# Fifteen tiles of the feed-forward's first product by seven block products (Strassen), with weight sums built in DRAM

## The chip, the cores and the metric

The kernel runs on one core of one Trainium2 chip. The metric is device time in microseconds (us). Every time below that is not a time of a whole run is read from one profiled execution of the kernel before.

## The reference, cut to what matters

One inference step of a decoder: 512 prompt tokens and 64 sample tokens (8 sequences of 8), 576 rows in all, 1024 features, float32. The part that the change rewrites is the last sub-layer:

```python
xn = rms_norm(x, g[4])
gate, up = jnp.split(xn @ w_ffn_in, 2, axis=-1)          # w_ffn_in: 1024 x (2 x 2816)
x = x + rms_norm((jax.nn.silu(gate) * up) @ w_ffn_out, g[5])   # w_ffn_out: 2816 x 1024
```

Ahead of it stand an in-projection of 1024 to 6144 columns, a gated convolution and a gated recurrence, their output projections and merge, and a cross-attention into 256 memory tokens, each with norms before and after.

## The kernel before

**Layout.** Activations stand with 128 features on the partitions and the 576 tokens along the free axis; the columns come as halves of 288 (`HN`), or, between the mix and the end, as half A (320 columns: the samples and half of the prompt) and half B (256 columns).

**Products.** TensorE works on pairs: `split` (L101) makes of a float32 tile a rounded high part on ScalarE (L102) and the rest on VectorE (L103), and `mm3` (L105) makes of each 128x128 block of weights three matmuls, high by high (L106), high by low (L107) and low by high (L108). A tile of 128 output features over 1024 input features is thus 8 x 3 matmuls for each half of the columns.

**Weight stream.** SyncE (SP) loads one 128x1024 tile of weights (512 KB, rows of 512 bytes) at L165 into `wraw` (5 buffers), and `w_prep` (L169) splits it into `whi` and `wlo` (4 buffers each). A step's products call for the split of the tile three steps ahead, and that for the load two further ahead:

```python
def w_prep(upto, dma_ahead=2):
    ...
    i = ptr["prep"]
    w_dma(i + dma_ahead)
    ...
    w_prep((w[0] if w else nextw) + 3)      # in run_steps, ahead of each step's products
```

The first tiles are split by ScalarE (L360) and GpSimd (L361).

**Stages.** Start (x loaded, normed and transposed); eight column tiles `c` of the in-projection (`in_u`, `in_hc`, `in_hh`, `in_gate`, `in_hb`: four weight tiles and the gate's blocks for each `c`); branches out and merge; mix; memory keys and values, queries, attention in an order written out by hand; feed-forward in; feed-forward out. In the in-projection GpSimd splits the gate's blocks (`gate_w`, L469 and L470), copies and clears small pieces (L485 to L492, L537, L538, L544, L585 to L593). GpSimd also issues the few transfers of activations to DRAM (L841, L943, L969, L1191, L1269), on a queue of its own, q0 in the profile; SyncE's loads are q1.

**Feed-forward in.** 22 column tiles `j`. Tiles 0 to 6 run half A ahead of half B's attention output (`ffn_half`); tiles 7 to 21 as two steps each, `ffn_gate` (L1226) and `ffn_up` (L1239), 2 x 48 matmuls of alternately 320 and 256 columns, PSUM tiles `mm` of two banks.

**Feed-forward out.** 8 output tiles `n`, each in three groups of k (8, 8 and 6 of the 22 tiles) that accumulate in PSUM, `ffo`; the last two tiles are done by halves, (6, A), (7, A), (6, B), (7, B), so that the end of half A (`rb_a`, `y_a`, `out_a`) stands among products of half B. `last` does tile 7 of half B with the sums of squares (L1379), the last scale (L1396) and the stores.

**Order.** The program is written in steps; a scheduler then orders each engine's own instructions by priority and by what it expects to be ready, so an instruction that waits for nothing can stand much earlier on its engine than it is written. Every engine runs its own list strictly in order.

Of the kernel before, what the change touches and what calls it, by code (L numbers as in the profile page):

```python
# [9 lines left out]
F32 = mybir.dt.float32  # L10
# [5 lines left out]
D = 1024  # L16
# [23 lines left out]
# Background work (ns) let in behind a step.  # L40
# [12 lines left out]
def decoder_step(  # L53
# [18 lines left out]
    # ---------------------------------------------------------------- storage  # L72
# [76 lines left out]
    # ---------------------------------------------------------------- weight stream  # L149
    wsrc = []  # L150

    def w_cols(w, r0, nk, c0, ncol, as_is=False):
        src = w[r0:r0 + nk * 128, c0:c0 + ncol].rearrange("(k p) c -> p k c", p=128)
        wsrc.append((src, nk, ncol, as_is))
        return len(wsrc) - 1
# [4 lines left out]
    def w_dma(upto):  # L160
        while ptr["dma"] <= min(upto, len(wsrc) - 1):
            i = ptr["dma"]
            src, nk, ncol, _ = wsrc[i]
            t = wraw_p.tile([128, 1024], F32, tag="wraw", name="wraw")
            nc.sync.dma_start(out=t[:, :nk * ncol].rearrange("p (k c) -> p k c", c=ncol), in_=src)  # L165
# [3 lines left out]
    def w_prep(upto, dma_ahead=2):  # L169
        while ptr["prep"] <= min(upto, len(wsrc) - 1):  # L170
# [5 lines left out]
            ptr["prep"] += 1  # L176
            if as_is:
                ready[i] = t
                continue
# [6 lines left out]
    # ---------------------------------------------------------------- program order  # L186
# [34 lines left out]
    # ---------------------------------------------------------------- constants  # L221
# [42 lines left out]
    def rows_rstd(o, j, m):  # L264
        """rs[:, j:j+m] from the sums of squares there; columns from o on are scratch."""
# [12 lines left out]
    def startup():  # L278
        log_exp()
        # x: token tiles, the first three of them ahead of everything else  # L280
# [49 lines left out]
        def sums(i):  # L330
            """rs[:, i]: sum of squares, one half of the columns on each engine."""
# [93 lines left out]
        # transposed vectors  # L425
# [47 lines left out]
    # ---------------------------------------------------------------- in-projection  # L473
# [145 lines left out]
    for c in range(KT):  # L619
# [10 lines left out]
        step(wi(0), *in_hb(c), budget=9000)  # L630

# [870 lines left out]
```

## Time and profile before

| what | us |
|---|---|
| three runs | 1180.17, 1181.19, 1181.98 (median 1181.19) |
| profiled execution, span from its first to its last instruction | 1179.4 |
| the median of the runs beyond that span | 1.8 |
| TensorE busy | 1159.2 (98%) |
| VectorE, ScalarE, GpSimd busy | 609.5, 555.2, 119.2 |

The profiled execution's time of its own is its span, 1179.4; the page gives no other, and the runs' times hold what lies around a span as well. All sums are made against 1179.4, and 1.8 is added to set a result beside the runs.

How to read the profile: TensorE is busy all the time but for a few us at the start and the end. The chain of work that ended last shows which engine the end waited for at each moment; idle time of the other engines costs nothing by itself.

### The profile page before, as it was taken

The numbers are of one execution on the slowest core, as the hardware profiler recorded it, in microseconds if no ns is written. First come the engines' busy times: TensorE is split into PE (matmuls) and PEld (weight loads), VectorE is DVE, ScalarE is ACT, GpSimd is POOL, SyncE is SP. The second block draws the span as 40 slices with busy tenths as digits, with TensorE's granted clock in tenths as the row PEclk, the third lists the DMA queues.
The fourth block names the chain that finished last, engine by engine and source line by source line (L and its number), as shares of the span: only waits on it lengthen the run. The fifth ranks groups of instructions, "written<-read, shape, count | busy, mean of one in ns | idle before, by whom it ended". The sixth has DMA issues, their size and how long they took to land.

```text
span 1179.4 us, 20915 instructions
## 1 busy us (share of the span) xinstructions
PE 1159.2 (98%) x8704; PEld 1139.8 (97%) x8704; DVE 609.5 (52%) x926; ACT 555.2 (47%) x924; POOL 119.2 (10%) x253
## 2 busy tenths in 40 slices
PE   6999999999999999999999999999999999999997
PEld 4999999999999999999998899999999999999997
DVE  6666555652223335787768768974323323212235
ACT  5665655652122226676567777764322222222233
POOL 5332222202000000113200000000000000000000
PEclk9999999999999999999999999999999999999999
DMA  8323222222323345566765775665333232232352
GB/s 234 92 86 90 73 77 86 72 85 85 90 73 89 93 149 164 175 190 203 226 212 197 228 224 149 207 179 158 109 100 89 83 90 67 81 86 81 92 159 90
DMA packets 234635, 150.76 MB, mean 128 GB/s; under 512 B 7817, under 2 KB 222873, under 8 KB 234539
## 3 DMA queue, kind: packets, MB, share of 16 engines
q1 hardware_dynamic: 231300, 141.03, 40.7%
q0 software_dynamic: 2432, 7.04, 1.6%
q10 hardware_dynamic: 806, 1.34, 0.4%
q8 instruction: 68, 1.11, 0.4%
q14 instruction: 29, 0.23, 0.1%
HBM read 139.99 MB, written 9.40 MB: 127 GB/s over the span
## 4 chain that ended last, share of the span: by engine, by line
PE 95%; DMA 2%; ACT 1%; DVE 1%; issue 0%; POOL 0%; SPq 0%; DVEq 0%
PE mm L106 29%; PE mm L107 29%; PE mm L108 29%; PE aux L1099 1%; PE aux L1083 1%; DMA wraw<-in_cache_mem_v_dram 1%; PE aux L106 1%; PE aux L107 1%; PE aux L108 1%; DMA wraw<-in_w_in_dram 1%; PE aux L831 0%; PE aux L385 0%; DMA wraw<-in_w_o_x_dram 0%; PE aux L768 0%; POOL wlo L361 0%
## 5 line engine op out<-in xcount | busy, mean ns | idle before, releaser
L106 PE MATMUL mm<-u,whi 128*128 128x288 f32 (+2 forms) x2506 | 745.7, 298 | 0.0
L108 PE MATMUL mm<-u,wlo 128*128 128x288 f32 (+2 forms) x2506 | 742.2, 296 | 1.1 <-POOL wlo L361 1.1
L107 PE MATMUL mm<-u,whi 128*128 128x288 f32 (+2 forms) x2506 | 741.8, 296 | 0.0
L108 PEld LDWEIGHTS mm<-u,wlo 128*128 128x128 f32 x2506 | 474.3, 189 | 1.7 <-POOL wlo L361 1.5
L107 PEld LDWEIGHTS mm<-u,whi 128*128 128x128 f32 x2506 | 474.5, 189 | 1.2 <-DVE u L389 0.3
L106 PEld LDWEIGHTS mm<-u,whi 128*128 128x128 f32 x2506 | 474.4, 189 | 1.0 <-ACT u L388 0.2
L102 ACT CAST whi<-wraw 128x1024 fp32r<-128x1024 f32 (+1 forms) x229 | 237.8, 1039 | 486.7 <-PE mm L107 301.0
L103 DVE TENSOR_TENSOR wlo<-wraw,whi 128x1024 fp32r<-128x1024 f32 (+1 forms) x229 | 277.6, 1213 | 323.9 <-ACT whi L102 320.4
L102 ACT CAST u<-u 128x320 fp32r<-128x320 f32 (+6 forms) x116 | 54.3, 500 | 68.2 <-DVE u L543 26.3
L103 DVE TENSOR_TENSOR u<-u,u 128x320 fp32r<-128x320 f32 (+6 forms) x116 | 60.2, 542 | 15.7 <-ACT u L102 15.5
L1252 DVE TENSOR_TENSOR u<-u,mm 128x320 f32<-128x320 f32 (+1 forms) x30 | 12.3, 451 | 64.1 <-PE mm L108 64.1
L103 DVE TENSOR_TENSOR u<-aux,u 128x512 fp32r<-128x512 f32 (+2 forms) x60 | 32.8, 585 | 3.8 <-ACT u L102 3.7
L102 ACT CAST u<-aux 128x512 fp32r<-128x512 f32 (+2 forms) x60 | 28.0, 515 | 5.7 <-DVE u L103 2.1
L106 PE MATMUL aux<-u,u 128*128 128x256 f32 (+1 forms) x96 | 27.8, 294 | 0.0
L108 PE MATMUL aux<-u,u 128*128 128x256 f32 (+1 forms) x96 | 27.6, 288 | 0.0
L107 PE MATMUL aux<-u,u 128*128 128x256 f32 (+1 forms) x96 | 27.6, 288 | 0.0
L841 POOL DMA_DIRECT2D x_s<-u x8 | 4.5, 561 | 227.1 <-DVE u L832 226.9
L673 DVE TENSOR_TENSOR u<-u,mm 128x576 f32<-128x576 f32 x8 | 6.0, 754 | 33.8 <-PE mm L108 33.8
L653 DVE TENSOR_TENSOR u<-u,mm 128x576 f32<-128x576 f32 x8 | 6.0, 755 | 30.1 <-PE mm L108 30.1
L496 DVE SCALAR_TENSOR_TENSOR u<-u,vecs,u 128x600 f32<-128x600 f32 x24 | 20.2, 842 | 2.5 <-ACT u L494 1.9
L590 DVE TENSOR_TENSOR u<-mm,u 128x64 f32<-128x64 f32 (+2 forms) x24 | 7.3, 352 | 27.1 <-PE mm L108 27.1
L720 DVE TENSOR_TENSOR u<-u,u 128x640 f32<-128x640 f32 (+1 forms) x24 | 18.6, 778 | 0.9 <-ACT u L719 0.9
(250 smaller groups left out, 951.4 us busy)
## 6 DMA issues: line engine op xcount, KB each, us to landing
wraw<-in_w_ffn_in_dram SPq DMA_DIRECT2D x58, 512.0 KB, 3.8
wraw<-in_w_in_dram SPq DMA_DIRECT2D x48, 512.0 KB, 3.8
wraw<-in_w_ffn_out_dram SPq DMA_DIRECT2D x20, 512.0 KB, 3.9
wraw<-in_w_mix_out_dram SPq DMA_DIRECT2D x16, 512.0 KB, 4.3
wraw<-in_w_kv_x_dram SPq DMA_DIRECT2D x16, 512.0 KB, 4.1
wraw<-in_w_q_x_dram SPq DMA_DIRECT2D x16, 512.0 KB, 4.3
wraw<-in_cache_mem_k_dram SPq DMA_DIRECT2D x16, 512.0 KB, 4.3
wraw<-in_cache_mem_v_dram SPq DMA_DIRECT2D x16, 512.0 KB, 4.4
```

The lines of the kernel that those rows point to most:

```text
L102: ACT.copy(hi, src)
L103: DVE.tensor_sub(lo, src, f(hi))
L106: PE.matmul(out, lhsT=wh, rhs=xh, start=start, stop=False)
L107: PE.matmul(out, lhsT=wh, rhs=xl, start=False, stop=False)
L108: PE.matmul(out, lhsT=wl, rhs=xh, start=False, stop=stop)
L496: DVE.scalar_tensor_tensor(uc[:, :NU], up[:, k:k + NU], wcb(k, c), uc[:, :NU], op0=ALU.mult, op1=ALU.add)
L590: DVE.tensor_mul(o, i, src if a else src.rearrange("p (b t) -> p b t", t=8))
L653: DVE.tensor_mul(both(t), both(t), box.pop("yr")[:, :, :HN])
L720: DVE.tensor_add(M[key][:, :n], M[key][:, :n], s[:, :n])
L1083: PE.transpose(ps[:, d * 256 + i * 128:d * 256 + (i + 1) * 128], kr[i][:, h * 256 + d * 128:h * 256 + (d + 1) * 128], ident)
L1099: PE.matmul(ps[0:m], lhsT=t[:, k * 64:k * 64 + m], rhs=src, **kw)
L1252: DVE.tensor_mul(t[:, hs(h)], t[:, hs(h)], ps[:, h, :w])
```

## The change

- **Feed-forward in, tiles 7 to 21.** Each tile's gate and up columns, the even and odd input tiles, and the left and right halves of the 576 columns make a 2x2 by 2x2 block product. It is done with seven block products in place of eight (`ffn_pair`): EG, s1, s2, OG, s3, s4, OU, each 4 k-tiles x 3 matmuls of 288 columns. EG, s2, s3 and OU accumulate one after the other in bank 0 of one PSUM tile (each is copied out or used before the next is added), s1 and s4 in bank 1, OG in an `aux` tile. Copies and sums behind them: p1, p5, p6 on ScalarE, p2, p7, p3, p4 on VectorE.
- **Sums of activations.** `x3_sums` builds four sums of the normed input in background work (VectorE and ScalarE), 4 times.
- **Sums of weights.** `s1` to `s4`, each 512 rows x 1920 columns in DRAM, are made from `w_ffn_in` by 32 DMAs of 128 rows (0.983 MB each) that GpSimd issues: 16 plain copies and 16 that add to what stands there (`accum_op`). They are written two behind each `c` of the in-projection and one behind each step pair of the branches.
- **Weight loads of that stage.** A 128x1024 tile now holds two blocks of 4 k-tiles and comes by two DMAs of 256 KB (`w_blocks`); 53 tiles in place of 30 for the fifteen `j`.
- **Feed-forward out.** k in groups of 7, 7 and 8; the first two groups follow right behind their `j` and are kept in SBUF (`fs`, copied by ScalarE, then added by VectorE); in the last group the weights of tiles 3 to 7 are kept, half A of tiles 3 to 7 is done first, then half B.

```diff
+    def w_blocks(srcs):
+        wsrc.append((srcs, 4 * len(srcs), 128, False))
...
             t = wraw_p.tile([128, 1024], F32, tag="wraw", name="wraw")
-            nc.sync.dma_start(out=t[:, :nk * ncol].rearrange("p (k c) -> p k c", c=ncol), in_=src)
+            n = nk * ncol // len(srcs)
+            for j, src in enumerate(srcs):
+                nc.sync.dma_start(out=t[:, j * n:(j + 1) * n].rearrange("p (k c) -> p k c", c=ncol), in_=src)
...
+            if as_is == "keep":
+                hi, lo = new(F32R, 2), new(F32R, 2)
+                for j in range(2):
+                    split(hi[j][:, 0:512], lo[j][:, 0:512], t[:, j * 512:(j + 1) * 512])
+                ready[i] = Halves(hi), Halves(lo)
+                continue
...
+    sums = {n: tc.dram_tile([512, DFF - NB * 128], F32, name=f"sum_{n}") for n in ("s1", "s2", "s3", "s4")}
+    def sum_task(op, n, src, i):
+        def go():
+            r = slice(i * 128, i * 128 + 128)
+            if src in sums:
+                a = sums[src][r, :]
+            else:
+                k = 2 * i + (src[0] == "O")
+                c = (src[1] == "U") * DFF
+                a = w_ffn_in[0][k * 128:(k + 1) * 128, c + NB * 128:c + DFF]
+            kw = {"accum_op": ALU.add} if op == "add" else {}
+            nc.gpsimd.dma_start(out=sums[n][r, :], in_=a, **kw)
+        return go
+    sum_tasks = deque(
+        sum_task(op, n, src, i)
+        for stage in ((("copy", "s1", "EU"), ("copy", "s3", "EG")), (("add", "s1", "OU"), ("add", "s3", "EU")),
+                      (("copy", "s2", "s3"),), (("add", "s2", "OU"),), (("copy", "s4", "s2"),), (("add", "s4", "OG"),))
+        for op, n, src in stage for i in range(4))
+    def sum_step():
+        if sum_tasks:
+            step([], sum_tasks.popleft(), budget=0)
...
         step(wi(0), *in_hb(c), budget=9000)
+        for _ in range(2):
+            sum_step()
...
         step([w_cols(w_rnn_out[0], 0, KT, n * 128, 128)], *br_rnn(n))
...
+        sum_step()
...
         step([w_cols(w_conv_out[0], 0, KT, n * 128, 128)], *br_conv(n))
+        sum_step()
...
+    def x3_sums(i):
+        def go():
+            a, b = x3f[2 * i], x3f[2 * i + 1]
+            DVE.tensor_sub(a[:, L], a[:, L], a[:, R])
+            DVE.tensor_sub(a[:, R], b[:, R], a[:, R])
+            DVE.scalar_tensor_tensor(b[:, R], a[:, L], -1.0, b[:, R], op0=ALU.mult, op1=ALU.subtract)
+            DVE.scalar_tensor_tensor(b[:, L], b[:, R], -1.0, b[:, L], op0=ALU.mult, op1=ALU.subtract)
+            for k, t in ((2 * i, a), (2 * i + 1, b)):
+                t_h[k], t_l[k] = new(F32R), new(F32R)
+                split(t_h[k][:, 0:T], t_l[k][:, 0:T], t[:, 0:T])
+            free(a, b)
+        return go
...
+    def product(W, b, ps, X, xs, first, last):
+        wh, wl = W
+        xh, xl, o = X
+        for i in range(4):
+            k, x = 4 * b + i, 2 * i + o
+            PE.matmul(ps, lhsT=wh[:, k, :], rhs=xh[x][:, xs], start=first and i == 0, stop=False, skip_group_check=True)
+            PE.matmul(ps, lhsT=wh[:, k, :], rhs=xl[x][:, xs], start=False, stop=False, skip_group_check=True)
+            PE.matmul(ps, lhsT=wl[:, k, :], rhs=xh[x][:, xs], start=False, stop=last and i == 3, skip_group_check=True)
...
+        def p6():
+            ACT.copy(FF["t"][:, R], FF["b"][0])
...
+        def p7():
+            DVE.scalar_tensor_tensor(FF["u"][:, L], FF["b"][0], -1.0, FF["u"][:, L], op0=ALU.mult, op1=ALU.subtract)
+        def p3():
+            t = FF["t"]
+            DVE.tensor_add(t[:, R], t[:, R], FF["b"][1])
+            ACT.activation(t[:, 0:T], t[:, 0:T], AF.Silu)
...
+            DVE.scalar_tensor_tensor(t[:, L], FF["b"][0], -1.0, t[:, L], op0=ALU.mult, op1=ALU.mult)
+            DVE.tensor_mul(t[:, R], t[:, R], u[:, L])
...
+        N, TT = (x3n_h, x3n_l), (t_h, t_l)
+        return [("EG", (*N, 0), L, 0, True, True, p1, begin), ("s1", (*TT, 0), L, 1, True, True, p5, None),
+                ("s2", (*TT, 1), R, 0, False, True, p6, None), ("OG", (*N, 1), L, 2, True, True, p2, None),
+                ("s3", (*TT, 0), R, 0, False, True, p7, None), ("s4", (*N, 1), R, 1, False, True, p3, None),
+                ("OU", (*TT, 1), L, 0, False, True, p4, None)]
+    def ffn_pairs(js):
+        todo = [(j, p) for j in js for p in ffn_pair(j)]
+        for n in range(0, len(todo), 2):
+            two = todo[n:n + 2]
+            w = w_blocks([block(p[0], j) for j, p in two])
...
-    kgroups = ((0, 8), (8, 8), (16, 6))
...
+    kgroups = ((0, 7), (7, 7), (14, 8))
...
+                fs[n] = new()
+                ACT.copy(both(fs[n]), ps[:, :, :HN])
+            else:
+                DVE.tensor_add(both(fs[n]), both(fs[n]), ps[:, :, :HN])
...
+                DVE.tensor_add(fs[n][:, hs(h)], fs[n][:, hs(h)], ps[:, h, :HW[h]])
...
+    def last(W):
+        k0, nk = kgroups[2]
+        p0, ps = sums_of([F["acc"][:, c0:c0 + m] for c0, m in htiles[1]]), auxt()
+        DVE.tensor_scalar(rs[:, 16:18], p0[:, 0:2], D * EPS, None, op0=ALU.add)
+        gemm(ps[:, 0:256], W, G, 1, k0, 4, True, False)
+        tok_out(6)
+        for i in range(3):
+            out_a(i, 1)()
+        gemm(ps[:, 0:256], [w[:, 4:, :] for w in W], G, 1, k0 + 4, 4, False, True)
+        fg, f1 = new(), fs[7][:, hs(1)]
+        DVE.tensor_add(f1, f1, ps[:, 0:256])
...
+    for part, js in enumerate((range(NB, 7), range(7, 14), range(14, KF))):
+        ffn_pairs(js)
+        if part < 2:
+            for n in range(KT):
+                step(wo(n, part), *ffo_part(n, part))
+                if sp:
+                    step([], sp.pop(0))
...
+    seq = [(n, (0, 1)) for n in range(3)] + [(n, (h,)) for h in range(2) for n in range(3, KT)]
+    after = {(3, (1,)): [rb_a], (4, (1,)): [y_a(0), y_a(1)], (5, (1,)): [y_a(2), y_a(3)],
+             (6, (1,)): [out_a(i, 0) for i in range(3)]}
```

The lines of the changed file are numbered anew: L513 is the DMA of `sum_task`, L387 and L405 are what L361 and L379 were, L495 and L496 the gate's split (L469, L470), L590 and L591 the scan's start (L537, L538), L543 and L545 the copies of u (L490, L492); L1345 to L1347 are the matmuls of `product`, L1357, L1360 and L1363 the copies p1, p5 and p6.

**GpSimd, start of the program.** Before, GpSimd stands like this between the first clears and the gate's blocks (u2 and u3 hold the gate's blocks):

```order
L379 TENSOR_SCALAR u2_91<-ident_76 128x512
L379 TENSOR_SCALAR u3_92<-ident_76 128x512
L361 TENSOR_TENSOR wlo_181<-wraw_113,whi_180 128x1024
L361 TENSOR_TENSOR wlo_304<-wraw_119,whi_303 128x1024
L361 TENSOR_TENSOR wlo_422<-wraw_121,whi_421 128x1024
```

Now, from the same place:

```order
L513 DMA sum_s1_95<-in_w_ffn_in_dram 128x1920
L387 TENSOR_TENSOR wlo_185<-wraw_117,whi_184 128x1024
L405 TENSOR_SCALAR u2_91<-ident_76 128x512
L405 TENSOR_SCALAR u3_92<-ident_76 128x512
L513 DMA sum_s1_95<-in_w_ffn_in_dram 128x1920
L387 TENSOR_TENSOR wlo_308<-wraw_123,whi_307 128x1024
L540 MEMSET u41_722 128x3
L639 MEMSET u46_859 128x2
L513 DMA sum_s1_95<-in_w_ffn_in_dram 128x1920
L387 TENSOR_TENSOR wlo_426<-wraw_125,whi_425 128x1024
L513 DMA sum_s1_95<-in_w_ffn_in_dram 128x1920
```

The first of the 32 DMAs stands ahead of the first split of weights, and the two clears L405 have moved behind that split. Further down the list, still in the first tiles `c`, the DMAs stand among the scan's start and the copies of u (u41 is the u of the second `c`):

```order
L513 DMA sum_s1_95<-in_w_ffn_in_dram 128x1920
L513 DMA sum_s3_97<-in_w_ffn_in_dram 128x1920
L591 COPY u35_588<-h0x_81 128x8
L543 COPY sto_84<-u41_722 128x24
L545 COPY sto_84<-u41_722 128x3
L513 DMA sum_s3_97<-in_w_ffn_in_dram 128x1920
L597 COPY sto_84<-u34_587 128x8
```

From the ninth on each DMA waits on the semaphore of the one issued eight earlier. The last of the 32 stands right ahead of the L545 of the fourth `c`: all are in the part of the list that belongs to the first four of the eight tiles `c`.

**ScalarE and TensorE, feed-forward in.** Before, a tile's Silu (L1236) stands behind one cast of weights, on a PSUM tile that nothing adds to afterwards:

```order
L102 CAST whi_10510<-wraw_10387 128x1024
L1236 ACTIVATE u1_10505<-mm_10456 128x320
L1236 ACTIVATE u1_10505<-mm_10456 128x256
L102 CAST whi_10573<-wraw_10450 128x1024
```

Now, for tile j = 10, whose PSUM tile is `mm_10503`:

```order
L1360 COPY u57_10506<-mm_10503 128x288
L102 CAST whi_10536<-wraw_10457 128x1024
L1363 COPY u52_10505<-mm_10503 128x288
L1357 COPY u46_10627<-mm_10625 128x288
```

The cast into `whi_10536` takes the buffer of `whi_10394`, four tiles back, which s2 reads. On TensorE the end of s2 and the start of s3 (which adds to the bank that L1363 copies) stand like this:

```order
L1346 MATMUL mm_10503<-u15_9272,whi_10394 128x288
L1347 MATMUL mm_10503<-u36_9271,wlo_10395 128x288
L1347 MATMUL mm_10625<-u12_8466,wlo_10500 128x288
L1345 MATMUL mm_10625<-u25_8514,whi_10499 128x288
...
L1346 MATMUL mm_10625<-u26_8570,whi_10499 128x288
L1347 MATMUL mm_10625<-u10_8569,wlo_10500 128x288
L1345 MATMUL mm_10503<-u30_9128,whi_10427 128x288
```

Between the last use of `whi_10394` and s3's first matmul there are eleven matmuls: the last of s2 and ten of the next tile's EG. In ten of the fifteen `j` it is ten of EG, in five (9, 11, 16, 18, 20) it is seven.

**TensorE and VectorE, the end.** Before, the sums of squares of half B (L1379) stand in the middle of tile 7, and VectorE has the eight operations of `y_a` (L1408, L1409) ahead of them, with one addition of squares (L1358) among them. Now, of VectorE, from the end of `rb_a` on (u17 holds the sums of squares):

```order
L810 SCALAR_TENSOR_TENSOR u28_12823<-u15_12822 128x320
L1509 TENSOR_TENSOR u54_9958<-u54_9958,mm_12829 128x256
L1572 TENSOR_TENSOR u55_12459<-u55_12459,u28_12823 128x640
L1572 TENSOR_TENSOR u38_12596<-u38_12596,u28_12823 128x640
L1522 TENSOR_TENSOR u17_12456<-u17_12456,u37_12854 128x256
...
L1573 TENSOR_TENSOR u36_12755<-u36_12755,u7_12618 128x640
L1509 TENSOR_TENSOR u5_10062<-u5_10062,mm_12909 128x256
L1522 TENSOR_TENSOR u17_12456<-u17_12456,u11_12934 128x256
```

and of TensorE, between tile 6 and tile 7 of half B:

```order
L108 MATMUL mm_12909<-u44_12402,wlo_12604 128x256
L1534 MATMUL aux_12940<-ident_76,u48_12896 128x128 x2
L1415 MATMUL aux_12945<-ident_76,u55_12459 64x128 x2
...
L1543 MATMUL aux_12969<-ones_f_77,u17_12456 128x1 x2
L106 MATMUL aux_12972<-u3_11522,whi_12658 128x256
```

The sums (L1543) now stand ahead of all products of the last tile, and need the squares of tile 6, whose addition is VectorE's last row above.

## Rows read from the trace of the kernel before

**Rows 1.** The page: the span, the engines' busy times, the chain that ended last.

```profile
span 1179.4 us, 20915 instructions
...
PE 1159.2 (98%) x8704; PEld 1139.8 (97%) x8704; DVE 609.5 (52%) x926; ACT 555.2 (47%) x924; POOL 119.2 (10%) x253
...
PE 95%; DMA 2%; ACT 1%; DVE 1%; issue 0%; POOL 0%; SPq 0%; DVEq 0%
```

**Rows 2.** Timeline of TensorE, three stretches: start, duration (us), instruction.

```profile
299.76 0.29 PE L106 MATMUL mm<-u,whi 128*128 128x288 f32 x1
...
303.06 0.29 PE L107 MATMUL mm<-u,whi 128*128 128x288 f32 x1
...
880.43 0.28 PE L106 MATMUL mm<-u,whi 128*128 128x256 f32 x1
...
883.19 0.28 PE L108 MATMUL mm<-u,wlo 128*128 128x256 f32 x1
...
884.18 0.31 PE L106 MATMUL mm<-u,whi 128*128 128x320 f32 x1
...
887.12 0.31 PE L108 MATMUL mm<-u,wlo 128*128 128x320 f32 x1
```

**Rows 3.** Groups of ScalarE's instructions, 430 to 990: count | busy us, mean ns.

```profile
L102 ACT CAST whi<-wraw 128x1024 fp32r<-128x1024 f32 x135 | 141.4, 1050 | 203.9 <-issue 124.1 <-PE mm L107 61.7 <-DMA wraw<-in_w_q_x_dram 5.2
...
L1236 ACT ACTIVATE u<-mm 128x256 f32<-128x256 f32 x12 | 4.5, 376 | 0.0
```

**Rows 4.** Chain of work that ended last, the end: start, duration, what.

```profile
1171.09 0.13 PE aux L108
1171.24 0.39 ACT u L1444
1171.68 0.62 PE aux L1379 x4
```

**Rows 5.** The same chain, the start.

```profile
3.39 6.24 DMA wraw<-in_w_in_dram
...
10.78 4.50 POOL wlo L361
```

**Rows 6.** DMA: the queue of GpSimd's transfers over the whole span (page).

```profile
q0 software_dynamic: 2432, 7.04, 1.6%
```

**Rows 7.** DMA queues in 751:752, then 752.5:753: packets, MB, share of 16 engines.

```profile
q1 hardware_dynamic: 589, 0.30, 105.3%
...
q0 software_dynamic: 34, 0.15, 81.3%
q1 hardware_dynamic: 34, 0.02, 11.4%
```

**Rows 8.** Busy time by stretch; last: TensorE clock, DMA share, GB/s.

```profile
33.00:118.00 85.00, 85.00 (x643) 84.64 (x642) 55.84 (x91) 51.83 (x79) 27.51 (x70) 1.00 0.30 87
0.00:118.00 118.00, 106.58 (x751) 102.85 (x752) 75.81 (x151) 68.65 (x120) 44.25 (x103) 1.00 0.44 125
```

**Rows 9.** Timeline of GpSimd: start, duration, instruction, idle time before it.

```profile
33.97 0.21 POOL L490 COPY sto<-u 128x24 f32<-128x24 f32 x1 [3.81 <-ACT u L488]
...
113.64 1.16 POOL L490 COPY sto<-u 128x24 f32<-128x24 f32 x1 [1.53 <-ACT u L488]
...
750.55 0.54 POOL L1191 DMA_DIRECT2D x2a_s<-u  x1 [99.61 <-DVE u L1220]
```

**Rows 10.** Timeline of the end: TensorE, VectorE and ScalarE.

```profile
1162.34 1.80 PE L1265 MATMUL aux<-ident,u 128*64 128x128 f32 x12
...
1159.99 1.56 DVE L1408 TENSOR_TENSOR u<-u,u 128x640 f32<-128x640 f32 x2
...
1162.94 0.42 DVE L1358 TENSOR_TENSOR u<-u,u 128x256 f32<-128x256 f32 x1
...
1157.37 0.52 ACT L748 ACTIVATE u<-aux,eps_t 128x320 f32<-128x320 f32 x1
...
1159.44 0.47 ACT L1354 ACTIVATE u<-mm,gT 128x256 f32<-128x256 f32 x1 [0.54 <-PE mm L108]
```

More of the change, by code (lines that the diff above doesn't have):

```diff
@@ L788, in post_tasks, with pre_tasks_wide, one @@
         return rstd_tasks(("f", h), h, ("rf", h), load) + [(2000, one(p)) for p in range(4)]
+    def pre_tasks_wide(h, gi, xf, oh, ol, done, load=False):
+        def one(p):
+            def go():
+                x = fb[p][h]
+                for j in range(2):
+                    k = 2 * p + j
+                    if xf[k] is None:
+                        xf[k], oh[k], ol[k] = new(), new(F32R), new(F32R)
+                    t = xf[k][:, hs(h)]
+                    DVE.scalar_tensor_tensor(t, x[:, w2(h, j)], gain(gi, k), M["rx", h][:, 0:HW[h]],
+                                             op0=ALU.mult, op1=ALU.mult)
+                    split(oh[k][:, hs(h)], ol[k][:, hs(h)], t)
+                done(p, h)
+                if p == 3:
+                    free(M.pop(("rx", h)))
+            return go
+        return rstd_tasks(("x", h), h, ("rx", h), load) + [(1500, one(p)) for p in range(4)]
     def pre_tasks(h, gi, oh, ol, done, load=False):
@@ L1174, in sa_fin @@
         free(t, S.pop("pad"), *box.pop("qs"))
[L1176 removed]
+    x3f, x3n_h, x3n_l = [None] * KT, [None] * KT, [None] * KT
     x1r = [[None] * 2 for _ in range(4)]
@@ new lines, in ffn_pairs, with pe @@
+    def ffn_pairs(js):
[3 more added lines that the diff above has]
+            w = w_blocks([block(p[0], j) for j, p in two])
+            for b, (j, (_, X, xs, bank, first, last, post, begin)) in enumerate(two):
+                def pe(W=None, b=b, X=X, xs=xs, bank=bank, first=first, last=last, begin=begin):
+                    if W is not None:
+                        FF["W"] = W
+                    if begin:
+                        begin()
+                    product(FF["W"], b, FF["b"][bank], X, xs, first, last)
+                step([w] if b == 0 else [], pe, post)
@@ L1319, in decoder_step @@
     sp = [spill(i, c4) for c4 in range(2) for i in range(2)]
-    for j in range(NB, KF):
-        step(wf(j, 0), *ffn_gate(j))
-        step(wf(j, 1), *ffn_up(j))
-        if sp:
-            step([], sp.pop(0))
     x2t, ft = [], []
@@ new lines, in wo @@
+    def wo(n, part, keep=False):
+        k0, nk = kgroups[part]
+        return [w_cols(w_ffn_out[0], k0 * 128, nk, n * 128, 128, keep=keep)]
+    sp = [spill(i, c4) for c4 in range(2) for i in range(2)]
+    for part, js in enumerate((range(NB, 7), range(7, 14), range(14, KF))):
[6 more added lines that the diff above has]
+    seq = [(n, (0, 1)) for n in range(3)] + [(n, (h,)) for h in range(2) for n in range(3, KT)]
@@ L1459, in decoder_step @@
+    after = {(3, (1,)): [rb_a], (4, (1,)): [y_a(0), y_a(1)], (5, (1,)): [y_a(2), y_a(3)],
+             (6, (1,)): [out_a(i, 0) for i in range(3)]}
     prev = None
+    kept = {}
     step([], log_exp)
     for n, hh in seq:
-        for part, (k0, nk) in enumerate(kgroups):
-            w = [w_cols(w_ffn_out[0], k0 * 128, nk, n * 128, 128)]
-            if (n, hh) == (7, (1,)):
-                step(w, last(part))
-            else:
-                step(w, *ffo(n, hh, part))
-            if part == 0 and prev and 1 in prev[1]:
-                step([], lambda n=prev[0]: tok_out(n))
-            for fn in after.get((n, hh, part), ()):
-                step([], fn)
@@ L1472, in decoder_step @@
-        if (n, hh) == (7, (0,)):
-            step([], lambda: (free(*[g[0] for g in gg]), x2_in()))
+        if hh != (1,):
+            pe, post = ffo(n, hh)
+            step(wo(n, 2, n == 3), lambda W, n=n, pe=pe: (kept.__setitem__(n, W), pe(W)), post)
+        elif n < KT - 1:
+            pe, post = ffo(n, hh)
+            step([], lambda n=n, pe=pe: pe(kept[n]), post)
+        else:
+            step([], lambda: last(kept[KT - 1]))
+        if prev and 1 in prev[1] and prev[0] != 6:
+            step([], lambda n=prev[0]: tok_out(n))
@@ L1474, in decoder_step @@
+        for fn in after.get((n, hh), ()):
+            step([], fn)
+        if n == 2:
+            step([], x2_in)
         prev = (n, hh)
```

168 lines of the change are left out of this document (92 added, 76 removed).

## The prediction

> **What bounds the kernel now.** I read the page first: TensorE is busy for 1159.2 of 1179.4 us, and the chain of work that ended last is 95% TensorE [rows 1]. So a matmul that is left out shortens the run by its interval, and everything else costs only what it makes TensorE wait. Second, TensorE's timeline, for the interval from one matmul's start to the next: 25 intervals of 288 columns in 3.30 us, 132 ns; 23 of 256 columns in 2.76 us, 120 ns; 20 of 320 columns in 2.94 us, 147 ns [rows 2]. Third, because the change adds 31 MB of DRAM traffic (32 x 0.983), the DMA views: over the first 118 us the 16 engines are busy 0.44 of the time, from 33 on 0.30 [rows 8].
>
> **The products.** Per tile j, eight products of 12 matmuls become seven. In the order of TensorE's instructions 1056 matmuls of 320 columns and 1056 of 256 go, and 1932 of 288 come (part of them because the two first groups of feed-forward out now run on halves of 288). 1056 x (0.147 + 0.120) = 282.0 us go, 1932 x 0.132 to 0.133 (what the rounding of the 3.30 us leaves open) = 255.0 to 257.0 come: a gain of 25.0 to 27.0. I take **-25.5**.
>
> **A new wait in each j.** s3 adds to bank 0, which ScalarE must first copy out (L1363). On ScalarE the cast of a weight tile stands right ahead of that copy, and the cast needs the buffer that s2 has just finished. From the start of s2's last matmul on that buffer: the matmul 0.29 [rows 2], the cast 1.05, the copy of 288 columns 0.40 (256 took 0.376) [rows 3], and three hand-overs of about 0.05 (TensorE to ScalarE 1171.09 + 0.13 to 1171.24, ScalarE to TensorE 1171.63 to 1171.68) [rows 4]: 1.89. TensorE's cover is that matmul's own interval and eleven more, 12 x 0.132 = 1.59, so it waits 0.30; in the five j with three matmuls less, 0.70. 10 x 0.30 + 5 x 0.70 = **+6.5**, between 0 (if the cast starts earlier than I think) and 10 (hand-overs of 0.1). The other banks have 12 to 22 matmuls of cover and no cast ahead. With the cover gone altogether each j would wait 1.9, 28 in all. Throughput is no bound: a j lasts 84 x 0.1325 = 11.1 us, in which ScalarE casts 3.5 tiles (3.7 us) and VectorE as many rests; 3.5 x 0.524 MB in 11.1 us is 165 GB/s, against 300 when the weight queue is alone [rows 7]. The activations' sums stand in background work on VectorE, which is half idle [rows 1]: 0.
>
> **The end.** TensorE now comes to the sums of squares (L1543) ahead of the last tile. From the end of (3, B): TensorE has rb_a's product (0.4), 72 matmuls of 256 columns (8.6) and the transposes (1.8 for twelve [rows 10] and three pairs of 0.25): 11.6 us. VectorE must wait for Ln, Exp and Square (3 x 0.5) and has two operations of 0.5, eight of y_a at 0.74 to 0.78, and four pairs of an addition of products and one of squares at 0.42; the last pair also waits for ScalarE's copy and square (0.47 + 0.38) [rows 10]. That is 0.4 + 1.5 + 1.0 + 6.0 + 3.4 + 0.9 = 13.2, 1.6 more than TensorE's. Behind the last product there is one more addition of 256 columns (0.42). **+2**, between 0.4 (VectorE works ahead while it waits) and 4.5 (ScalarE's copies for the stores stand ahead).
>
> **The weight sums.** They have no price by themselves, since nothing waits for them until far later; their price is what they take from the weight stream. Both the written places and the scheduler's differ: in GpSimd's list the first DMA stands ahead of the first weight split and the last one in the fourth tile c, where before the copy of that u ran at 113.64 [rows 9]. So 31 MB pass in about 115 us, beside the stage's own traffic.
>
> What does one cost? GpSimd issues one in 0.54 us [rows 9]: nothing. Its queue moved 7.04 MB in 1.6% of 1179.4 = 18.9 us of all engines, 0.373 MB/us [rows 6], so a copy of 0.983 MB takes 2.6 us of all 16 engines. No row shows a DMA that adds. It cannot do less than the copy, so 2.6 is the lower bound; as it reads two operands for one written, I take twice, 5.2, as the upper one. Sixteen of each: 85 to 127 us. I take the middle, 3.9 for an adding DMA: 106.
>
> What is there? To about 118 us the stage's own loads use 0.44 x 118 = 52 us of the engines [rows 8], which leaves 118 - 3 - 52 = 63. The weights that TensorE may live on, 8 tiles (5 raw, 3 split ahead, by the program) of 0.524 MB at 0.30 MB/us [rows 7], give another 14. So 106 us of sums stand against 77: **+29** of wait, 8 for the lower bound, 50 for the upper one.
>
> Would the sums not simply come last? The rows say they win. In 751:752 the weight queue is alone and has all of the engines; in 752.5:753, beside a write from GpSimd's queue, its 512-byte packets get 11% and the other's 81% [rows 7], 0.02 MB in half a microsecond where 82 GB/s are needed (0.524 MB for 48 matmuls). Each engine seems to take a packet of each queue in turn, and a packet of the sums is a row of 7680 bytes.
>
> The Trainium skill, "DMA: Bandwidth & Descriptors", section "Queues, rings and completion order", has each engine go round-robin between the queues at packet granularity, which agrees with the 11% and 81% of those rows. The Trainium skill, "Collectives: The Full Stack", section "The bandwidth ceiling: the fold count and why AG ≠ RS ≠ AR", says that an add by DMA is slower because it needs two source reads, with a measured ratio of 1.93; no run here shows it. By that the sums would take 42 + 81 = 123 us, the wait would be 46, and the result some 17 us above mine.
>
> **The start.** The first DMA of the sums is issued at about 1.7, and competes with the load of the first weight tile, which is on the chain (3.39 to 9.63), as is GpSimd's split behind it [rows 5]: up to one copy's 2.6 us, **+2.5**. It is zero only if it is slow to begin.
>
> **Sum.** 1179.4 - 25.5 + 6.5 + 2 + 2.5 = 1164.9 without contention; with it 1164.9 + 29 = 1193.9. The median of the runs lay 1.8 above the profiled span: **1196**.
>
> **Rivals.**
> - *The sums are hidden (faster).* Their bytes go by while the engines idle. For it: 0.56 of the engines' time is free up to 118 us; an adding DMA may cost little more than a copy; GpSimd's own waits (for the copy of u, the scan) space the sums, so that the stream recovers between them, and up to eight may still be outstanding when the list goes on, past 118. Against it: the 11%, and the first 33 us, in which the engines are already busy for 0.8 of the time (0.44 x 118 less 0.30 x 85 of 33) [rows 8]. With 0 to 8 us of wait: 1165 to 1173, 1167 to 1175 as a median. It decides below an adding DMA of about 2.8 us (sums of 88 us, 11 over, about what the other terms save), or if the queue of the sums doesn't hold back the weights.
> - *Adding DMAs run at half the copy's rate or worse.* Then 50 us and more: 1164.9 + 50 + 1.8 = 1217, and 1240 with 6.6 us each. For it the two reads; against it that an engine that only moves may have reads to spare.
> - *The change's saving does not arrive.* If every s3 waited 1.9, a third of the saving would remain even without contention: 1164.9 + 22 + 1.8 = 1189. Against it the ten matmuls of cover.
> - *No change that can be measured.* 12 to 17 us of wait balance the saving; a coincidence.
>
> **How the numbers follow.** The sums hold back the weights by 15 to 55 us: 0.46 (1182 to 1222). They are hidden or nearly so: 0.38. Worse than that: 0.09. The rest, around equality: 0.07. About 0.2% (2.4 us) is what a measurement of this kernel can tell from no change. Faster: the hidden case and a little of the rest, 0.40; same 0.06; slower 0.54. The predicted time is that of the likeliest, 1196, for itself 1182 to 1222; as the hidden case holds most of the other chance, the range takes it in, from 1166, and leaves the worse cases out: 1166 to 1222.
>
> **What would show it.** Right: TensorE's idle time in the first 130 us is some 30 us, ended by the loads or splits of weights, in stretches where q0 moves 0.3 MB/us and q1 a few tens of GB/s; the adding DMAs' packets take longer than a copy's of the same size; the engines' busy share between 33 and 118 is near 1 instead of 0.30. Each step: between s2 and s3 TensorE waits 0.3 to 0.7 for L1363; at L1543 it waits 1 to 4 for VectorE; the stage of the pairs is shorter by 25 less 6. Wrong: the in-projection takes as long as before, with the engines' share around 0.6, and the adding DMAs as fast as copies; then the result is near 1168. It is also wrong if the scheduler's places don't hold in time because GpSimd waits on its queue so long that the scan's start behind it (L591) holds up VectorE and, a tile later, TensorE: waits on L591 would show that.

## The result, and the profile after

The changed kernel takes 1219.47 us (median), the kernel before beside it 1181.29: ratio 1.0341, 95% interval 1.03 to 1.0382. It is slower, as forecast, and inside the forecast range, but by 38 us where 15 were predicted. Its four runs lie between 1217.4 and 1230.0, so a single run of a kernel with waits like its own tells little below some ten us. The profiled execution spans 1215.6 us, 36.2 more than before.

The page of the changed kernel: engines' busy time, TensorE and the DMA engines by 40 slices of 30.4 us (tenths), the two main queues (packets, MB, share of 16 engines) and the chain:

```profile
span 1215.6 us, 20941 instructions
PE 1152.9 (95%) x8524; PEld 1120.4 (92%) x8524; DVE 672.7 (55%) x1033; ACT 597.6 (49%) x981; POOL 141.9 (12%) x285
...
PE   4968699999999999999999999999999999999996
...
PEclk9979799999999999999999999999999999999999
DMA  8999993222332235556676676465434543355602
...
q1 hardware_dynamic: 249812, 149.95, 41.8%
q0 software_dynamic: 6144, 38.50, 11.4%
...
PE 83%; DMA 9%; ACT 3%; DVE 2%; issue 1%; another core or an unknown queue 1%; POOL 0%; SPq 0%; DVEq 0%; ACTq 0%
```

TensorE's busy time is 6 us shorter than before and 180 matmuls are gone, as they should. The holes are in the first six slices, where the DMA engines are full; the chain now holds 9% DMA instead of 2% [rows 1]. The same by stretches (busy us of TensorE, its weight loads, VectorE, ScalarE, GpSimd, then clock, DMA share, GB/s):

```profile
0.00:33.00 33.00, 16.39 (x81) 12.80 (x82) 19.30 (x57) 14.72 (x37) 18.95 (x33) 1.00 0.83 257
33.00:60.00 27.00, 26.66 (x205) 26.22 (x204) 16.97 (x42) 18.24 (x29) 16.80 (x36) 1.00 1.05 314
60.00:90.00 30.00, 19.02 (x124) 18.79 (x123) 11.19 (x16) 7.38 (x13) 9.12 (x16) 0.77 1.04 231
90.00:120.00 30.00, 27.48 (x207) 27.24 (x206) 13.87 (x18) 12.95 (x20) 12.14 (x26) 1.00 1.03 267
120.00:150.00 30.00, 17.02 (x117) 17.02 (x118) 7.20 (x13) 11.07 (x14) 4.80 (x14) 0.77 1.03 285
150.00:180.00 30.00, 27.59 (x196) 27.35 (x195) 20.23 (x27) 18.71 (x28) 12.36 (x27) 0.94 1.01 246
180.00:240.00 60.00, 60.00 (x454) 60.00 (x453) 37.83 (x50) 35.49 (x54) 18.22 (x42) 1.00 0.28 80
```

The share of the DMA engines from 33 on was 0.30 [rows 8]; it is 1.0 until 170, where the last of the sums lands, and at 180 it is back. The waits of TensorE in the first 300 us (total, times, longest), and of ScalarE's casts in 33 to 180:

```profile
PE mm L106 <- ACT u L622: 15.5, 1, 15.5
PE mm L106 <- ACT u L541: 13.4, 2, 11.0
PE aux L411 <- DVE x L378: 11.0, 2, 10.7
```

```profile
ACT whi L102 <- DMA wraw<-in_w_in_dram: 44.5, 7, 17.3
```

What came last each time is a weight tile, but TensorE did not wait for the tile itself. The chain shows the load, under way for 36.65 us, and ScalarE's timeline what stood behind it:

```profile
41.07 36.65 DMA wraw<-in_w_in_dram
```

```profile
77.80 1.04 ACT L102 CAST whi<-wraw 128x1024 fp32r<-128x1024 f32 x1 [17.30 <-DMA wraw<-in_w_in_dram]
78.75 0.75 ACT L541 COPY u<-mm 128x64 f32<-128x64 f32 x3
...
131.34 1.04 ACT L102 CAST whi<-wraw 128x1024 fp32r<-128x1024 f32 x1 [17.15 <-DMA wraw<-in_w_in_dram]
132.30 0.63 ACT L622 COPY u<-mm 128x576 f32<-128x576 f32 x1
```

ScalarE stands 17 us at a cast whose tile has not landed. Behind the cast on its list stands the copy (L541, L622) that empties a PSUM tile, and 0.05 us after the copy's end, at 79.56 and 132.98, TensorE goes on. By 68.3 eight tiles had been cast and TensorE had used six; by 117.2 it was thirteen and eleven.

**Where the 36.2 us are.** TensorE's first product, before and after:

```profile
12.97 0.63 PE L106 MATMUL mm<-u,whi 128*128 128x320 f32 x1
...
16.41 0.61 PE L106 MATMUL mm<-u,whi 128*128 128x320 f32 x1
```

It starts at 16.41 instead of 12.97: +3.4. From 33 on TensorE stands still three times, for 11.1 us from 68.3, 15.7 from 117.2 and 2.6 from 153.6 (from one matmul's start to the next, less one interval): +29.4. After each of these waits it runs at the lower of its two clock levels for a while (granted clock 0.77 in 60 to 90). TensorE's timeline after the first wait:

```profile
79.56 0.61 PE L106 MATMUL mm<-u,whi 128*128 128x288 f32 x1 [10.98 <-ACT u L541]
79.96 0.44 PE L107 MATMUL mm<-u,whi 128*128 128x288 f32 x1
...
85.00 0.40 PE L107 MATMUL mm<-u,whi 128*128 128x288 f32 x1
85.24 0.30 PE L108 MATMUL mm<-u,wlo 128*128 128x288 f32 x1
85.37 0.29 PE L106 MATMUL mm<-u,whi 128*128 128x288 f32 x1
```

From 79.96 to 85.24 the interval is 0.24 us, 1.2 GHz, in place of 0.132 [rows 2]; the 52 longer intervals in the three places add 5.9 us. That makes 38.7; a single interval of 0.63 at 49.1 and other small breaks are the rest of the 39.4 us by which TensorE is late through all of the branches. In the attention 1.3 more are lost (the last addition L778, L720 before, starts at 802.8 instead of 762.0). The rest of the program, the feed-forward, gains only 40.7 - 36.2 = 4.5, where 17 were forecast.

**The sums' queue.** A packet is the piece that a DMA engine moves at a time. Two stretches of the changed kernel: plain copies of the sums in 32:36, and only adding DMAs in 66:76.

```profile
q0 software_dynamic: 195, 1.30, 79.4%
...
q0 software_dynamic: 293, 2.00, 96.7%
q1 hardware_dynamic: 294, 0.15, 7.2%
```

Copies move 1.30 / (0.794 x 4) = 0.41 MB/us, adding DMAs 2.00 / (0.967 x 10) = 0.207: half. A copy of 0.983 MB costs 2.4 us of the engines, an adding DMA 4.75. The Trainium skill, "Collectives: The Full Stack", section "The bandwidth ceiling: the fold count and why AG ≠ RS ≠ AR", has 1.93 for the ratio of a collective that copies to one that adds, and puts it down to the second source that an add reads; the trace, with 1.98 for a copy and an adding DMA, agrees. And beside them the weight stream gets one packet of 512 bytes for each packet of 7680: 294 to 293, 0.15 MB in 10 us, 15 GB/s where 82 are needed.

**The feed-forward.** ScalarE, then TensorE, around the start of one tile's s3 in the changed kernel:

```profile
937.50 1.05 ACT L102 CAST whi<-wraw 128x1024 fp32r<-128x1024 f32 x1 [1.83 <-PE mm L1346]
938.45 0.39 ACT L1363 COPY u<-mm 128x288 f32<-128x288 f32 x1
```

```profile
938.62 0.29 PE L1346 MATMUL mm<-u,whi 128*128 128x288 f32 x1
938.90 0.40 PE L1345 MATMUL mm<-u,whi 128*128 128x288 f32 x1
939.14 0.30 PE L1346 MATMUL mm<-u,whi 128*128 128x288 f32 x1
939.27 0.29 PE L1347 MATMUL mm<-u,wlo 128*128 128x288 f32 x1
```

The cast stands ahead of p6, s3 starts when p6 is done, as foreseen: 0.28 from the matmul before instead of 0.13, and the next interval is 0.24 as well. The wait of 0.15 thus costs 0.26. But s3 is not the only one. Over the stage of the pairs (918 to 1150) there are 63 such places, some four in each j, and by the starts of the matmuls they cost 17.4 us. The waits of TensorE's weight loads (PEld) there, those of 0.15 us and more, show who is late:

```profile
PEld aux L1345 <- ACT whi L102: 2.9, 5, 0.6
PEld mm L1345 <- ACT u L1360: 2.7, 10, 0.4
PEld mm L1345 <- DVE u L1373: 2.3, 9, 0.7
PEld mm L1345 <- ACT u L1363: 1.7, 8, 0.2
PEld mm L1347 <- DVE wlo L103: 1.7, 5, 0.4
```

p6 (L1363) is one of five; p5 (L1360), the last addition in bank 1 (L1373), and the casts and rests of the weights themselves are the others. Of the 63, with the short ones, 10 wait for p6 and cost 2.3 us; 15 wait for L1373 (3.5 us), 10 for p5 (3.1), 10 for casts and rests (4.9), 15 for p7 (L1369, 2.4), and three for others.

### The profile page after: what moved, and what is told of

Same layout as the page of the kernel before. It is cut to its first block, busy times and chain, and to the rows that moved or that the text cites. A ratio compares the mean times of both kernels' runs of the same rounds, so it can differ in the third digit from the quotient of the medians.

```text
span 1215.6 us, 20941 instructions
## 1 busy us (share of the span) xinstructions
PE 1152.9 (95%) x8524; PEld 1120.4 (92%) x8524; DVE 672.7 (55%) x1033; ACT 597.6 (49%) x981; POOL 141.9 (12%) x285
## 3 DMA queue, kind: packets, MB, share of 16 engines
q0 software_dynamic: 6144, 38.50, 11.4%
## 4 chain that ended last, share of the span: by engine, by line
PE 83%; DMA 9%; ACT 3%; DVE 2%; issue 1%; another core or an unknown queue 1%; POOL 0%; SPq 0%; DVEq 0%; ACTq 0%
PE mm L106 21%; PE mm L107 21%; PE mm L108 21%; DMA wraw<-in_w_in_dram 7%; PE mm L1345 4%; PE mm L1347 3%; PE mm L1346 3%; ACT whi L102 1%; PE aux L1175 1%; PE aux L1159 1%; PE aux L106 1%; PE aux L108 1%; PE aux L107 1%; DVE wlo L103 1%
## 5 line engine op out<-in xcount | busy, mean ns | idle before, releaser
L106 PE MATMUL mm<-u,whi 128*128 128x288 f32 (+2 forms) x2024 | 604.5, 299 | 30.0 <-ACT u L622 15.5
L108 PE MATMUL mm<-u,wlo 128*128 128x288 f32 (+2 forms) x2024 | 600.9, 297 | 1.1 <-POOL wlo L387 1.1
L107 PE MATMUL mm<-u,whi 128*128 128x288 f32 (+2 forms) x2024 | 600.8, 297 | 0.0
L102 ACT CAST whi<-wraw 128x1024 fp32r<-128x1024 f32 (+1 forms) x245 | 254.4, 1040 | 449.5 <-PE mm L107 224.3
L103 DVE TENSOR_TENSOR wlo<-wraw,whi 128x1024 fp32r<-128x1024 f32 (+1 forms) x245 | 297.1, 1213 | 270.4 <-ACT whi L102 260.0
L106 PEld LDWEIGHTS mm<-u,whi 128*128 128x128 f32 x2024 | 384.3, 190 | 32.4 <-ACT u L622 15.7
L107 PEld LDWEIGHTS mm<-u,whi 128*128 128x128 f32 x2024 | 384.6, 190 | 1.8 <-DVE u L415 0.6
L108 PEld LDWEIGHTS mm<-u,wlo 128*128 128x128 f32 x2024 | 384.3, 190 | 1.7 <-POOL wlo L387 1.5
L1345 PE MATMUL mm<-u,whi 128*128 128x288 f32 x360 | 110.0, 310 | 1.0 <-DVE u L1373 0.5
L1346 PE MATMUL mm<-u,whi 128*128 128x288 f32 x360 | 105.4, 294 | 0.0
L1347 PE MATMUL mm<-u,wlo 128*128 128x288 f32 x360 | 102.6, 296 | 0.5 <-DVE wlo L103 0.5
L102 ACT CAST u<-u 128x576 fp32r<-128x576 f32 (+6 forms) x117 | 58.8, 531 | 66.7 <-DVE u L596 26.2
L1345 PEld LDWEIGHTS mm<-u,whi 128*128 128x128 f32 x360 | 67.2, 187 | 9.9 <-ACT u L1360 2.7
L103 DVE TENSOR_TENSOR u<-u,u 128x576 fp32r<-128x576 f32 (+6 forms) x117 | 65.2, 578 | 12.4 <-ACT u L102 12.3
L1347 PEld LDWEIGHTS mm<-u,wlo 128*128 128x128 f32 x360 | 66.4, 188 | 1.7 <-DVE wlo L103 1.7
L1346 PEld LDWEIGHTS mm<-u,whi 128*128 128x128 f32 x360 | 67.6, 188 | 0.0
L103 DVE TENSOR_TENSOR u<-aux,u 128x512 fp32r<-128x512 f32 (+2 forms) x60 | 32.8, 585 | 4.5 <-ACT u L102 4.5
```

What stands on the lines that cost most here:

```text
L102: ACT.copy(hi, src)
L103: DVE.tensor_sub(lo, src, f(hi))
L106: PE.matmul(out, lhsT=wh, rhs=xh, start=start, stop=False)
L107: PE.matmul(out, lhsT=wh, rhs=xl, start=False, stop=False)
L108: PE.matmul(out, lhsT=wl, rhs=xh, start=False, stop=stop)
L1345: PE.matmul(ps, lhsT=wh[:, k, :], rhs=xh[x][:, xs], start=first and i == 0, stop=False, skip_group_check=True)
```

## Experiments

**1. Without the sums.** The blocks s1 to s4 are loaded from `w_ffn_in`.

```diff
+    sum_tasks.clear()
...
-        if name in sums:
-            src = sums[name][:, (j - NB) * 128:(j - NB + 1) * 128].rearrange("(k p) c -> p k c", p=128)
-        else:
+        name = {"s1": "EU", "s2": "OU", "s3": "EG", "s4": "OG"}.get(name, name)
+        if True:
```

> All of the change without the 32 DMAs of the weight sums: the blocks s1 to s4 are read from columns of w_ffn_in in their place, by the same loads (the sums are left out of the computation). If the sums' traffic is the whole of the 40.7 us that the changed kernel is late when it reaches the feed-forward, the time is 1219.5 - 40.7 = 1179, and 1177 to 1181. If the loads of two 256 KB halves, the scheduler's other order or the feed-forward itself are a part of it, it stays above 1185. By the sum on record without contention it would be 1164; the trace of the changed kernel already speaks against that (the feed-forward gains 4.5 us, not 17).

1178.22 us beside 1181.89; ratio 0.9969, interval 0.9956 to 0.9982. TensorE has no wait between 33 and 300 us. So the 32 DMAs cost 41 us, and all else together gains 3 to 4.

**2. Adding DMAs as copies.**

```diff
-            kw = {"accum_op": ALU.add} if op == "add" else {}
+            kw = {}
```

> The 16 adding DMAs are plain copies of the same size (the sums are left out; all else as changed). Theory A (the adding DMA moves at half a copy's rate: 591 ns for a packet of 7680 bytes, against about 298): the sums take about 78 us of all engines instead of 115, the budget of 77 us is just met, and the wait shrinks from 39 to 4 to 12 us: 1183 to 1191. Rival (what costs is the number of DMAs, their place in GpSimd's list, or their waits on the one eight earlier): the time stays near 1219.

1197.91 us in one run: 21.6 less than the changed kernel, 19.7 more than without sums. The doubled length of the adding DMAs is half of the price, not most of it: my 4 to 12 us for the rest were too few. The first product is 3.4 us late, one wait of 12 us stands at 95.6, one of 0.9 at 48.9, and the lower clock behind them adds 2.7. The long one is again a cast that waits 17.6 us for its load, ahead of L541.

**3. Packets of 512 bytes.**

```diff
-    sums = {n: tc.dram_tile([512, DFF - NB * 128], F32, name=f"sum_{n}") for n in ("s1", "s2", "s3", "s4")}
+    sums = {n: tc.dram_tile([KF - NB, 512, 128], F32, name=f"sum_{n}") for n in ("s1", "s2", "s3", "s4")}
...
-            nc.gpsimd.dma_start(out=sums[n][r, :], in_=a, **kw)
+            nc.gpsimd.dma_start(out=sums[n][:, r, :].rearrange("a p c -> p a c"), in_=a, **kw)
```

> The sums are stored as fifteen blocks of 512 x 128 each, so that every packet of the 32 DMAs has 512 bytes instead of 7680; all else as changed. Theory A (each engine takes one packet of each queue in turn): the weight stream gets every second packet, some 100 GB/s beside adding DMAs and more beside copies, where it needs 82, so TensorE waits little: 1179 to 1187, although the sums take as long or longer than before. Rival B (capacity alone: the engines are full and any order costs the same): packets of 512 bytes need more time (at least 3.3 us for a copy, 6.5 for an adding DMA, 157 in all) and the wait grows by 40: 1255 to 1265.

1229.99 us in one run: neither. Two stretches of its queues, 60:90 and 98:115, both with adding DMAs alone, and TensorE's busy time:

```profile
q0 software_dynamic: 7096, 3.60, 94.5%
q1 hardware_dynamic: 4549, 2.30, 38.6%
...
q0 software_dynamic: 5767, 3.03, 137.9%
q1 hardware_dynamic: 377, 0.18, 5.6%
```

```profile
60.00:90.00 30.00, 30.00 (x228) 30.00 (x227) 18.34 (x26) 19.67 (x27) 14.88 (x19) 1.00 1.34 198
90.00:120.00 30.00, 8.91 (x68) 8.68 (x66) 0.44 (x1) 0.00 (x0) 10.12 (x17) 0.68 1.34 223
```

In 60:90 the packets of the adding DMAs have 0.5 KB, the weights get 77 GB/s, and TensorE does not wait at all: taking turns by packets decides what the weights get, as theory A says. From 33 to 180 no cast waits for a load. Yet TensorE stands still from 98.6 to 124.8 and from 153.4 to 170.1, and the waits in 33:180 show another cause:

```profile
DVE u L596 <- POOL u L591: 55.3, 3, 31.4
PE mm L106 <- ACT u L541: 42.3, 2, 25.9
POOL sum_s L513 <- DMA sum_s<-in_w_ffn_in_dram: 37.8, 8, 8.2
```

GpSimd stands at DMAs of the sums that wait for the one issued eight earlier. Behind them on its list stands the scan's start (L591); VectorE's scan (L596) waits for that, ScalarE's split and its copies (L541) for the scan, and TensorE for the copies. SyncE waits for a rest (L103) that stands behind the scan and issues no load, so in 98:115 the weight queue is nearly empty. An adding DMA moves only 0.13 MB/us in such packets (3.60 / 28.4), so the sums last until 201 instead of 170, and GpSimd's waits grow with them. The copies also went in packets of 4 KB (the queue joins them; its first stretch 20:33 holds 475 packets with 1.87 MB), which the edit did not intend. So the run confirms the turns by packets, and shows a second way in which the sums can stop TensorE.

**4. The sums alone**, in the kernel before.

> The kernel before with the 32 DMAs of the sums added at the same places of the program and nothing else of the change (two tiny transfers that read the sums are added so that they are kept). If the traffic is the cause by itself: 1181.3 + 37 to 42, 1218 to 1223, with TensorE's wait in the in-projection. If the price needs the rest of the change (the order of the weight splits), it is well below 1210.

1230.49 us in one run, 48.6 more than before and above the range expected: the traffic does it without the rest of the change (four waits, 37 us, and 7 for the lower clock). It lies beside the slowest run of the changed kernel, 1230.0, so whether it costs more there is not shown.

**5. The sums held apart.**

```diff
+        def go():
+            nc.gpsimd.dma_start(out=sums[n][i * 128:i * 128 + 1, 0:8], in_=f(anchor()[0:1, 0:8]))
+            sum_task("copy", n, parts_of[n][0], i)()
+            sum_task("add", n, parts_of[n][1], i)()
...
-        for _ in range(2):
-            sum_step()
+        sum_step(lambda c=c: vv[c])
```

> The changed kernel with the 32 DMAs held apart: the sums are made in sixteen pairs of a copy and an adding DMA, and each pair is tied to a value of its place in the program by a transfer of 32 bytes that GpSimd issues ahead of it (one pair behind each c of the in-projection, then one behind every second step pair of the branches). Nothing of the computation is left out. Theory A (the wait came from the sums standing close together; a pair takes 2.4 + 4.7 us of the engines in every 25 us, and the weights in hand last 51): no wait is left, the time is that of the run without sums, 1178, and 1176 to 1181. Rival (GpSimd, held up by its own DMA waits, delays the scan behind it, or any adding DMA costs the weight stream its length): 16 x 7 us partly shows, 1185 or more.

1178.88 us; ratio 0.9975, interval 0.9964 to 0.9985: as without sums. The same bytes, the same adding DMAs, and no wait:

```profile
33.00:118.00 85.00, 85.00 (x643) 84.66 (x642) 55.18 (x90) 51.61 (x78) 31.55 (x79) 1.00 0.55 144
118.00:240.00 122.00, 122.00 (x920) 122.00 (x920) 73.43 (x102) 74.68 (x109) 34.92 (x80) 1.00 0.58 152
```

**6. The same pairs, not held apart.** The transfer of 32 bytes, which experiment 5 adds ahead of each pair, is left out.

> The sums in the same sixteen pairs as in the run held apart, at the same places of the program, but without the transfers of 32 bytes that tie them there, so that the scheduler moves all of them ahead again, into the first four tiles c. Nothing of the computation is left out. If it was the distance between them that took the wait away, it is back: 1212 to 1225. If it was the order (each adding DMA right behind its copy, so that GpSimd waits between them), the time stays near 1179.

1212.0 us in one run: the waits are back. It is the distance between the DMAs that takes them away, not their order. They are of both kinds: in the first, 15.3 us from 48.8, a cast waits 10.6 us for its load; in the last, 11.4 us from 140.5, VectorE's scan waits 16.4 us for its start on GpSimd, which stands at a DMA of the sums.

**7. Copies first in the feed-forward**, without sums. p1 and p5 are edited as p6 is.

```diff
...
+            PE.matmul(ps, lhsT=wl[:, k, :], rhs=xh[x][:, xs], start=first and i == 0, stop=False, skip_group_check=True)
+            PE.matmul(ps, lhsT=wh[:, k, :], rhs=xh[x][:, xs], start=False, stop=False, skip_group_check=True)
+            PE.matmul(ps, lhsT=wh[:, k, :], rhs=xl[x][:, xs], start=False, stop=last and i == 3, skip_group_check=True)
...
         def p6():
-            ACT.copy(FF["t"][:, R], FF["b"][0])
+            with tc.high_priority(offset=300):
+                ACT.copy(FF["t"][:, R], FF["b"][0])
```

> The run without sums (they are left out of the computation), and in the feed-forward the copies p1, p5 and p6 get a higher priority and a product's last matmul is one on the high part of the weights, so that L1363 stands ahead of the cast on ScalarE in every j. The trace of the changed kernel shows 57 broken intervals in the stage of the pairs, 0.26 us each with the interval behind it, some four in each j. Theory: the wait of s3 for p6 goes (15 x 0.26), and with it a part of the others: 1174, 1171 to 1176. Rival: the cast that now stands behind the copy makes another product's first weights late, and the broken interval only moves: 1177 to 1180.

1167.84 us; ratio 0.9881, interval 0.9866 to 0.9895: 10.4 less than without sums, more than I expected of it. The waits of the weight loads in the stage of the pairs (870 to 1110; L1362 is p5) are then:

```profile
PEld mm L1345 <- ACT u L1362: 3.0, 15, 0.2
PEld mm L1345 <- ACT u L1366: 0.4, 2, 0.2
```

The waits for casts and rests are gone, and of those for p6 (now L1366) two are left. p5 is now waited for once in every j; the last addition in bank 1 (now L1376) still is too, but for less than the 0.15 us that are listed. The broken intervals of the stage cost 7.7 us here.

**8. and 9. Each of the two edits alone**, without sums.

> The run without sums (they are left out), and of the two edits that brought 10 us only the order of the three matmuls: low part first, so that the last matmul of a product reads the high part. In the order of ScalarE the cast still stands ahead of L1363 in part of the j. If the order on ScalarE is what counts: part of the gain, 1171 to 1176. If the order of the matmuls itself makes the weights' buffers or loads come earlier: 1168.

The order of the matmuls alone: 1176.92 us in one run, 1.3 less than without both, and within the spread of that kernel's runs (1176.8 to 1179.1).

> The run without sums (they are left out), and of the two edits only the priority of the copies p1, p5 and p6; in the order of ScalarE the cast still stands ahead of L1363 in most of the j. If the order on ScalarE is what counts: little gain, 1175 to 1179. If the priority alone is enough: 1168 to 1170.

The priority of the copies alone: 1175.62 us in one run, 2.6 less. Neither does it alone. On ScalarE p6 follows a cast without a pause in all 15 j of the changed kernel, in 7 with the order of the matmuls alone, in 15 with the priority alone, and in none with both.

**10. Sums held apart and copies first.**

> Both: sums in pairs tied to their places, copies first. Nothing of the computation is left out. If the two causes are apart, the time is that of the run without sums and with copies first: 1174, 1171 to 1177, faster than both kernels. If GpSimd's waits or the adding DMAs still cost something, it is 1180 or more.

1168.49 us beside 1181.56; ratio 0.9891, interval 0.9875 to 0.9908. All of the reference is computed, and this version is faster than both kernels, 1.1% faster than the one before.

## Why the prediction was right in direction and wrong in size

- **Fewer matmuls, -25.5.** Nothing speaks against it: 180 matmuls are gone, and with the two obstacles removed (experiment 10) the span is 1165.4, against 1164.9 "without contention". That nearness is partly luck: the first DMA's 2.5 and the 6.5 of s3 are not in that run, and some 8 us of broken intervals that I had not counted are.
- **"A new wait in each j", +6.5.** This step failed, and it is the largest part of the miss. The wait of s3 for L1363 is real, but small: 10 times, 2.3 us. What is wrong is that only s3 waits: "the other banks have 12 to 22 matmuls of cover and no cast ahead" and "throughput is no bound". Casts and rests stand in the order of ScalarE and VectorE ahead of p5, of L1373 and of a product's own first weights, and every one of those can be late by a little; with the broken interval behind it each costs about 0.3. Measured: 63 waits and 17.4 us in place of 6.5, and experiment 7 gave 10.4 us back.
- **The end, +2.** Right: TensorE waits 1.7 at L1543 for L1522, where 1.6 were worked out. In its timeline of the changed kernel:

```profile
1201.56 0.61 PE L1543 MATMUL aux<-ones_f,u 128*128 128x1 f32 x4 [1.70 <-DVE u L1522]
```

- **The start, +2.5.** Right in its mechanism; 3.4. The first weight tile lands at 13.0 instead of 9.63, and the load of x, which the term did not name, is as late.
- **"They win".** Right, and stronger than the rows of before showed: 15 GB/s are left to the weights, one packet each in turn.
- **+29 for the sums.** The waits add up to 29.4, but the agreement hides errors that cancel. The adding DMA takes 4.75 us, near the upper bound, and not the middle of 3.9; by the same budget that would have been about 40. And the budget is no good model. It takes the list as done by 118, while the sums ran to 170, for GpSimd itself was held up with TensorE. It gives TensorE all 8 tiles to live on, while it stood still with two split tiles unused, because ScalarE's copy stood behind the cast of a later one. For plain copies (experiment 2) it gave 8, and the waits were 13. What counts is how close together the DMAs stand: apart, the same 115 us of transfers cost nothing (experiment 5); close together, they cost 33 to 41 (experiment 6, the changed kernel). Whether L541 ahead of the cast would shorten the waits, no run shows. The point "below 2.8 us for an adding DMA" from which the hidden case should hold falls with it: copies of 2.4 us still cost 19.7.
- **No term for the clock.** After each of the three waits the lower clock cost another 1.6 to 2.6 us, 5.9 in all, and no term of the sum had it.

So of the 21.7 us between the forecast span (1193.9) and the measured one, 12.5 are in the feed-forward (10.9 of them the broken intervals), 5.9 the clock after the waits, 1.3 the attention, and 2.0 the start, the waits themselves and small breaks. What the attention loses, and 1.6 us in the feed-forward, stay unexplained.

Three figures of the rivals do not come out of their own terms, and nothing hangs on them: 6.6 us for each adding DMA give 1237, not 1240; 2.8 us give sums of 86 and 9 over, not 88 and 11; and with 22 us for s3 nothing of the saving would remain (1189 is above 1181), not a third.

That the scheduler moved the 32 DMAs ahead was read from the order and holds: written at a distance of some 13 us, they are issued between 1.6 and 156.6. The rival of a faster result named the right conditions (sums spaced, so that the stream recovers); GpSimd's own waits just don't provide them. The last sign of being wrong, waits on L591, shows in the changed kernel only once (4.8 us of VectorE, with no wait of TensorE beside it), but it is what costs most in experiment 3 and a part of experiment 6.

## What to carry to other kernels

Traffic that nothing waits for is not free: price it by what it does to the stream beside it, packet by packet, and look for the first instruction that waits for that stream and at what stands behind it on its engine; the tiles in hand are no measure. An engine that waits to issue a transfer also holds up all the work behind it. If a scheduler may move transfers that depend on nothing, tie them to a value of the place where they belong. And where a loop is cut into shorter products, look at every wait between them, in the order of the engines that serve them: a copy that frees a bank belongs ahead of a cast that is wanted three tiles later.

## What the runs showed of the hardware that was not expected

- An adding DMA from DRAM to DRAM moves 0.207 MB/us on all engines in packets of 7680 bytes, a copy 0.41; in packets of 512 bytes an adding DMA moves 0.13.
- GpSimd's queue joins the 512-byte rows of a plain copy into packets of 4 KB, and not those of an adding DMA. A copy from sum to sum, 983,040 bytes in one piece, went as 16 packets of 61,440 bytes.
- A weight load that starts 0.12 to 0.22 us late makes one interval of TensorE 0.05 to 0.15 us longer and the next one 0.11.
- After 11 us without work TensorE took 22 intervals of 0.24 us, 5.3 us, before it was back at 0.132.
